# The opening of a decoder layer: identity turnings on TensorE before x arrives, each tile of x scaled behind its own root, and the norm's factors loaded behind the first four tiles

## The chip, the cores and the metric

The kernel runs on one NeuronCore of a Trainium2 chip. The metric is the device time of one execution in microseconds (us), as the median of several runs. All times in this document are in us unless ns is written. The engines are PE (TensorE, matrix products and transposes), ACT (ScalarE), DVE (VectorE), POOL (GpSimd) and SP (SyncE, which issues most of the transfers). Each engine works its own queue in order; a queue stops at an instruction whose operands aren't there, and everything behind it waits too.

## The reference

One layer of a hybrid decoder, on 1024 tokens of width 1024 behind 16 learned meta tokens:

```python
h = concat([pad, meta_tokens, x])
h = h + 0.5 * swiglu(rms_norm(h, ffn1_norm), ffn1_w_in, ffn1_w_out)     # first half-step FFN
u = rms_norm(h, mix_norm) @ w_in
o = concat([hgrn2(...u...), stick_breaking(...u...)])                  # two groups of heads
h = h + o @ w_out
h = h + 0.5 * swiglu(rms_norm(h, ffn2_norm), ffn2_w_in, ffn2_w_out)     # second half-step FFN
return h[:, pad + meta:, :]

def rms_norm(x, gain):
    return x * rsqrt(mean(x * x, axis=-1) + 1e-6) * gain
```

Only the first line of real work matters here: the norm of the first FFN, `rms_norm(h, ffn1_norm)`, and the first products with `ffn1_w_in`. Everything is float32 and is computed to about that accuracy.

## The kernel before, in words

**The whole.** The kernel goes through the layer in order: first FFN in, first FFN out, mixing norm and projections, the heads, `w_out`, second FFN. Every float32 product is made of three passes: each operand is split into a rounded high part and a low part, and PE multiplies high by high, low by high and high by low. The two FFN products of 512-token halves use a Strassen-like scheme over 2 x 2 blocks with seven products instead of eight; its block operands are called B11, B21, T1 to T4 and B22. A group of 12 matmuls (four slices of 128 in depth, three passes each) is one such block product of one weight block with one operand.

**The opening** (`open_tokens`, from line 790) makes the operands of the first FFN. x is 1024 x 1024; the first 512 tokens are four row tiles of 128 x 1024 (`ra[0]` to `ra[3]`), the others are `rb[0]` to `rb[3]`. For each row tile:

- `row_sum` (lines 757 to 764): the sum of squares along each row, on ACT (line 764, an activation and a read of its accumulator) or on DVE (line 761, the same in one product).
- `row_root` (lines 766 to 770): a square root on ACT (line 769) and a reciprocal on DVE (line 770).
- `row_scale` (lines 772 to 776): DVE multiplies the tile by it, in one piece or in two halves of 512 columns.

Then `turned` (lines 778 to 788) transposes on PE: for each row tile in order, each of the named column blocks, as a product with the identity (line 785), into PSUM tiles `xps` that hold one column block k of all four row tiles. `first(k, ...)` (lines 832 to 836) multiplies such a PSUM tile by the norm's factor `g[k]`, which is `ffn1_norm` laid out by partitions (`g1`, 128 x 8): ACT makes the rounded high part (line 835), DVE the low part (line 836). Column blocks 0 to 3 make B11, 4 to 7 make B21. Line 854 and `spare` (line 830) make a plain scaled copy (`b11`) of blocks 0 and 1, after which their PSUM tiles are free; the transposes of blocks 6 and 7 go to the same two PSUM banks.

**The weights' side.** `fast_in` (from line 350) gives generators, one for each of eight column tiles of `ffn1_w_in`. `order` lists them by pairs. The first and second `next` of a generator each make one weight operand: a load of a 256 KB block issued by SP (line 370), a cast to the high part on ACT (line 360), a difference to the low part on DVE (line 362). The third `next` does the first group of 12 matmuls (operand B11, line 450) and a copy of its result on ACT (line 474), the fourth the second group (operand B21). So `order[0]` and `order[1]` are the first weight blocks of the first two generators, `order[2]` and `order[3]` their second blocks.

**What sets the order.** In `open_tokens` the order on ACT, DVE and SP is that of the program text (a manual schedule), and on PE it is so through the whole stage. POOL's order, and ACT's, DVE's and SP's outside this function, is planned by the framework. SP issues transfers in text order too: the four tiles `ra`, two weight blocks, the four tiles `rb`, a third weight block, the meta tokens, and further weight blocks. Eight transfers of these queues can be in flight, since each takes one of eight semaphores; the issue after those waits for the landing of the transfer that had the semaphore before.

**Constants.** `setup` (from line 69) makes the identity (DVE memset, then line 79 on POOL), constants, and a first square root on ACT (line 87). It collects the small loads in a list; the first of them, g1, is issued at once on ACT's queue (line 104): 1024 elements of four bytes, each to its own place. `masks_blank` (line 120) fills a tile on DVE from which POOL cuts masks (lines 129 and 133). Line 1824 in `run` makes `ng1`, the negative of g1, on DVE; it is first read at line 879, some steps later (`combine`).

Of the kernel before, what the change touches and what calls it, by code (L numbers as in the profile page):

```python
# [11 lines left out]
F32 = mybir.dt.float32  # L12
# [8 lines left out]
P = 128  # L21
# [27 lines left out]
class Block:  # L49
# [19 lines left out]
    def setup(self):  # L69
        nc, a = self.nc, self.a  # L70
        self.loads = []
        self.const = c = self.pool("const")
        c.tile([P, 368], F32, name="base")
        self.pool("edge", side="right").tile([P, 504], F32, name="edge")
        self.dram = self.pool("scratch", space=DRAM)

        self.ident = c.tile([P, P], F32, name="ident")
        nc.vector.memset(self.ident, 1.0)
        nc.gpsimd.affine_select(
            out=self.ident, in_=self.ident, pattern=[[-1, P]],  # L80
            compare_op=ALU.is_equal, fill=0.0, base=0, channel_multiplier=1,
        )
        self.ones_d = c.tile([P, P], F32, name="ones_d")
        nc.vector.memset(self.ones_d, 1.0 / D)
        self.eps = c.tile([P, 1], F32, name="eps")
        nc.vector.memset(self.eps, EPS)
        nc.scalar.activation(c.tile([P, 1], F32, name="root"), self.eps, AF.Sqrt)

        self.g1 = self.column(a["ffn1_norm"][0], KT, "g1")
        self.gm = self.column(a["mix_norm"][0], KT, "gm")  # L90
        self.g2 = self.column(a["ffn2_norm"][0], KT, "g2")
        self.og = self.column(a["hgrn_out_norm"][0], 4, "og")
        self.l0 = self.column(a["hgrn_lb_logits"][0], 4, "l0")
        self.l1 = self.column(a["hgrn_lb_logits"][1], 4, "l1")
        self.qg, self.kg, self.qg8 = (c.tile([P, 1], F32, name=x) for x in ("qg", "kg", "qg8"))
        for h in range(2):
            s = slice(64 * h, 64 * h + 64)
            self.loads.append((self.qg[s], a["sb_q_norm"].rearrange("a d -> d a")))
            self.loads.append((self.kg[s], a["sb_k_norm"].rearrange("a d -> d a")))
        self.mx, self.lb, self.lbc = (c.tile([P, 4], F32, name=x) for x in ("mx", "lb", "lbc"))  # L100
        self.masks = c.tile([P, len(LEVELS), P], U8, name="masks")
        self.ss = c.tile([P, 9, 2], F32, name="ss_x")
        self.ng1 = c.tile([P, KT], F32, name="ng1")
        nc.scalar.dma_start(*self.loads.pop(0))

    def setup_rest(self):

# [682 lines left out]
    def open_tokens(self, ops, opened, prepare, rows_at, ev, operands):  # L790
# [9 lines left out]
        nc, x = self.nc, self.a["x"][0]  # L800
# [3 lines left out]
        junk = [rp.tile([P, D], (BF16, U8)[i], name=f"junk{i}") for i in range(2)]  # L804
        order = [q for i in range(0, len(opened), 2) for _ in range(2) for q in opened[i : i + 2]]

        def rows_in(r0):
            got = []
            for i in range(4):
                row = rp.tile([P, D], F32, tag="row", name="row", bufs=8)  # L810
                nc.sync.dma_start(row, x[r0 + i * P : r0 + i * P + P])
                got.append(row)
            return got
# [12 lines left out]
        kept = {}  # L826
# [5 lines left out]
        def first(*ks):  # L832
            for k in ks:
                hi, lo = (t[:, k % 4, :] for t in ops[("B11", "B21")[k // 4]])
                nc.scalar.mul(hi, kept[k], g[k])  # L835
                stt(lo, kept[k], g[k], hi.bitcast(F32), ALU.mult, ALU.subtract)  # L836

        ra = rows_in(0)
        self.masks_blank(sd)
        for i in range(3):  # L840
            self.row_sum(ra[i], i, junk, nc.vector if i == 1 else nc.scalar)
            self.row_root(ra[i], i)
        for i in range(3):
            self.row_scale(ra[i], i)
        self.row_sum(ra[3], 3, junk, nc.scalar)
        self.row_root(ra[3], 3)
        self.row_scale(ra[3], 3, 2)
        next(order[0])
        next(order[1])
        rb = rows_in(512)  # L850
        meta = rp.tile([META, D], F32, name="meta")
        kept.update(self.turned(ra, range(6), "bbccdd"))
        first(0, 1, 2, 3)
        nc.vector.tensor_scalar_mul(b11[0], kept[0], g[0])
        spare(1)
        next(order[2])
# [4 lines left out]
        next(order[1])  # L861
        kept.update(self.turned(ra, (6, 7), "bb"))
        first(6, 7)
        next(order[3])

        def turn_b22():
# [907 lines left out]
    def run(self):  # L1774
        nc, tc, a = self.nc, self.tc, self.a
# [20 lines left out]
        with ExitStack() as c0:  # L1796
            with ExitStack() as c1:
# [8 lines left out]
                with tc.manual_schedule(engines={nc.tensor.engine}), ExitStack() as c2:  # L1806
# [14 lines left out]
                    operands(xa, ("B11", "B21"))  # L1821
                    self.pin = self.pool("pin1", 1, PSUM, c2)
                    self.t_bufs, self.in_bufs = 2, 10
                    nc.vector.tensor_scalar_mul(self.ng1, self.g1, -1.0)

                    def ahead_of_time(pool):

# [66 lines left out]
                    first, hooks, steps_ahead = 32, 54, 58  # L1894
# [272 lines left out]
                with tc.manual_schedule(engines={nc.tensor.engine}):  # L2167
# [7 lines left out]
                    with ExitStack() as c2:  # L2175
                        self.att.append(self.pool("att1", ctx=c2))
                        tag = self.proj_tags[0]
# [214 lines left out]
```

## Time and profile before

| | |
|---|---|
| median of three runs | 1959.63 |
| the three runs | 1960.16, 1959.63, 1957.4 |
| the profiled execution | 1959.65 |
| its span, first to last instruction | 1957.9 |
| PE busy | 1919.8 (98% of the span) |
| DVE busy | 1390.4 (71%) |
| ACT busy | 849.6 (43%) |
| POOL busy | 450.5 (23%) |

The 1.75 between the profiled execution's time and its span lie around the instructions. Where rows of the profile are quoted, they read as follows. In a timeline: start in us from the span's start, duration, engine, line of the kernel, instruction, output<-input by the program's names, shape, how many in a row (x4), and in brackets how long the engine had been idle and who ended that. An engine with a q (SPq, ACTq) is its issue of a transfer. In the chain of waits: start, duration, engine, tile and line of the work that the end of the span depended on. In the view of one tile: line, engine, instruction, count, shortest/median/longest duration in ns, first and last start. In the table by stretches: the stretch, its length, busy time (and count) of PE, PE's weight loads, DVE, ACT and POOL, the clock of PE, the share of the transfer engines, GB/s. Matmul durations in the trace overlap; the rate is read from their starts.

The profile's first 40th (0 to 49 us) has PE busy for 7 tenths, every other 40th for 9 tenths or more. PE's first instruction starts at 11.

### The profile page before, as it was taken

To read this page: it belongs to the slowest core of one execution; us is meant where nothing else is said; L and a number is where in the kernel's file an instruction comes from. 1 tells how busy PE (TensorE), PEld (TensorE's weight loads), DVE (VectorE), ACT (ScalarE), POOL (GpSimd) and SP (SyncE) were. 2 spreads that over 40 slices of the span, in tenths; PEclk is the share of its full clock that TensorE was granted. 3 is DMA by queue.
4 is the path that set the end of the run, shared out by engine and by line. 5 is a ranking of instruction groups with operands and counts; after the bars stand their busy time and mean duration, and the time that the engine had idled before them with its cause. 6 is when DMAs were issued, how large, how long until landed. Compare 5 with 4: busy or idle time off the path is not lost.

```text
span 1957.9 us, 30218 instructions
## 1 busy us (share of the span) xinstructions
PE 1919.8 (98%) x10607; PEld 1616.6 (83%) x10607; DVE 1390.4 (71%) x2184; ACT 849.6 (43%) x1711; POOL 450.5 (23%) x625
## 2 busy tenths in 40 slices
PE   7999999999999999999999999999999999999999
PEld 6888888788888888888898978887888888888887
DVE  7977877877678665467777766677567767766774
ACT  6523443334444544356666635433232332344443
POOL 3010100001000003133333332210544645530000
PEclk9999999999999999999999999999999999999999
DMA  7356887758965315865454177655634444469473
GB/s 213 93 165 170 253 272 243 233 203 291 375 221 188 127 54 144 193 170 148 128 148 121 57 253 225 161 208 183 198 115 140 128 131 121 132 243 318 154 231 113
DMA packets 381687, 355.54 MB, mean 182 GB/s; under 512 B 129040, under 2 KB 284560, under 8 KB 381536
## 3 DMA queue, kind: packets, MB, share of 16 engines
q1 hardware_dynamic: 359728, 288.98, 48.7%
q0 software_dynamic: 20768, 64.63, 9.5%
q8 instruction: 84, 1.38, 0.3%
q14 instruction: 67, 0.55, 0.1%
q10 hardware_dynamic: 1040, 0.00, 0.0%
HBM read 237.95 MB, written 115.57 MB: 181 GB/s over the span
## 4 chain that ended last, share of the span: by engine, by line
PE 89%; DVE 4%; DMA 3%; ACT 2%; issue 1%; POOL 1%; SPq 1%; DVEq 0%; ACTq 0%; POOLq 0%
PE o L732 21%; PE qb L450 18%; PE qa L450 12%; PE qc L450 12%; PE proj L249 5%; PE proj L251 4%; PE proj L250 4%; PE flip L1495 2%; PE wo L250 1%; PE wo L249 1%; PE wo L251 1%; PE mq L1001 1%; PE oacc L1572 1%; PE oacc L1570 1%; DMA oT<-oD 1%
## 5 line engine op out<-in xcount | busy, mean ns | idle before, releaser
L450 PE MATMUL qb<-T,wh 128*128 128x512 f32 x1056 | 344.6, 390 | 1.3 <-ACT T L309 0.8
L450 PEld LDWEIGHTS qb<-T,wh 128*128 128x128 f32 x1056 | 198.1, 188 | 46.4 <-issue 2.5
L450 PE MATMUL qa<-B,wh 128*128 128x512 f32 x696 | 226.7, 390 | 0.3 <-ACT B L835 0.2
L249 PE MATMUL proj<-xh,wh 128*128 128x512 f32 (+2 forms) x640 | 213.2, 333 | 2.6 <-ACT st L1142 1.3
L732 PE MATMUL o<-t,w 128*128 128x512 f32 x924 | 211.8, 390 | 0.7 <-DVE u L543 0.7
L251 PE MATMUL proj<-xl,wh 128*128 128x512 f32 (+2 forms) x640 | 210.2, 328 | 0.8 <-DVE xl L1957 0.8
L250 PE MATMUL proj<-xh,wl 128*128 128x512 f32 (+2 forms) x640 | 210.1, 328 | 0.0
L732 PE MATMUL o<-parts 128*128 128x512 f32 x924 | 209.6, 389 | 0.0
L450 PE MATMUL qb<-T,wl 128*128 128x512 f32 x528 | 205.5, 389 | 0.0
L732 PEld LDWEIGHTS o<-t,w 128*128 128x128 f32 x924 | 172.8, 188 | 37.8 <-ACT sgm L981 1.1
L732 PEld LDWEIGHTS o<-parts 128*128 128x128 f32 x924 | 173.5, 188 | 36.0
L362 DVE TENSOR_TENSOR wl<-s,wh 128x512 fp32r<-128x512 f32 x160 | 165.6, 1035 | 50.8 <-ACT wh L360 49.9
L360 ACT CAST wh<-s 128x512 fp32r<-128x512 f32 x160 | 99.2, 622 | 188.5 <-PE qb L450 141.1
L450 PEld LDWEIGHTS qa<-B,wh 128*128 128x128 f32 x696 | 130.5, 188 | 28.0 <-DVE B L836 0.5
L360 ACT CAST wh<-raw 128x512 fp32r<-128x512 f32 x120 | 74.4, 621 | 155.8 <-PE qc L450 111.4
L450 PE MATMUL qa<-B,wl 128*128 128x512 f32 x348 | 135.4, 389 | 0.0
L249 PEld LDWEIGHTS proj<-xh,wh 128*128 128x128 f32 x640 | 120.8, 189 | 15.0 <-ACT st L1142 2.2
L251 PEld LDWEIGHTS proj<-xl,wh 128*128 128x128 f32 x640 | 120.7, 189 | 12.3 <-DVE xl L1957 1.2
L250 PEld LDWEIGHTS proj<-xh,wl 128*128 128x128 f32 x640 | 120.8, 189 | 10.1
L450 PE MATMUL qc<-B,wh 128*128 128x512 f32 x352 | 115.1, 390 | 2.3 <-DVE u L543 2.3
L450 PE MATMUL qc<-T,wh 128*128 128x512 f32 x352 | 117.0, 394 | 0.0
L450 PEld LDWEIGHTS qb<-T,wl 128*128 128x128 f32 x528 | 99.1, 188 | 20.2
(393 smaller groups left out, 3819.4 us busy)
## 6 DMA issues: line engine op xcount, KB each, us to landing
raw<-in_ffn_w_in_dram SPq DMA_DIRECT2D x176, 256.0 KB, 4.0
raw<-in_ffn_w_out_dram SPq DMA_DIRECT2D x112, 256.0 KB, 4.5
w2in<-both SPq DMA_DIRECT2D x28, 512.0 KB, 3.4
raw<-in_w_in_dram SPq DMA_DIRECT2D x25, 512.0 KB, 5.2
ks<-kD SPq DMA_DIRECT2D x32, 260.0 KB, 4.8
wout<-both SPq DMA_DIRECT2D x16, 512.0 KB, 3.7
wh<-w2in SPq DMA_DIRECT2D x27, 256.0 KB, 3.1
wl<-w2in SPq DMA_DIRECT2D x27, 256.0 KB, 3.1
```

The costliest lines, as they stand in the source:

```text
L249: nc.tensor.matmul(ps, wh[:, s], xs, start=k == 0, stop=False)
L250: nc.tensor.matmul(ps, wl[:, s], xs, start=False, stop=False)
L251: nc.tensor.matmul(ps, wh[:, s], xl[:, k, c0 : c0 + n], start=False, stop=k == nk - 1)
L360: nc.scalar.copy(hi, src)
L362: self.block_lo = nc.vector.tensor_sub(lo, src, hi.bitcast(F32))
L450: nc.tensor.matmul(ps, a[:, k, :], b[:, k, :], start=start and k == 0 and i == 0, stop=k == 3 and i == 2, skip_group_check=True,)
L732: nc.tensor.matmul(banks[bank][m], y[:, m * P : (m + 1) * P], z, start=start and at == 0 and e == 0, stop=q == nq - 1 and e == 2, skip_gro ...
L1001: nc.tensor.matmul(ps[at : at + 32, :], self.xm[:, 4 * h + k, :], got[i, h][:, k, :], start=h == 0 and k == 0, stop=h == 1 and k == 3, til ...
L1495: self.nc.tensor.transpose(ps[:m, j, :], src[:, s0 : s0 + m], self.ident)
L1570: nc.tensor.matmul(o[:, c], vj, w[0], start=j == 0, stop=False, skip_group_check=True)
L1572: nc.tensor.matmul(o[:64, c], vj[:, :64], w[1], start=False, stop=end, skip_group_check=True)
```

## The change

- g1's load leaves ACT's queue in `setup` and becomes SP's fifth issue, behind the four tiles `ra` and ahead of the first weight block.
- PE gets 30 transposes of the identity at the head of its queue, into the four quarters of one PSUM tile (`warm`, one of the two buffers of tag `qd`), whose content nobody reads.
- The sums: tiles 0, 1 and 3 are now summed on ACT and tile 2 on DVE (before: 0, 2 and 3 on ACT, 1 on DVE). Each tile is scaled right behind its own root, not after all three roots.
- The first weight operand of the second generator (`order[1]`) and the loads of `rb` come in the text behind the turning of column blocks 0 to 5 and `first(0, 1, 2, 3)`, not ahead of them: on ACT and DVE its cast and its low part are now queued behind the four B11 products, and ahead of `b11`. On SP the order of the loads stays.
- `ng1` is made after `first(6, 7)` and no longer at line 1824.

```diff
@@ setup
         self.ng1 = c.tile([P, KT], F32, name="ng1")
-        nc.scalar.dma_start(*self.loads.pop(0))
@@ open_tokens
         ra = rows_in(0)
+        nc.sync.dma_start(*self.loads.pop(0))
+        warm = self.pin.tile([P, 512], F32, tag="qd", name="warm", bufs=2)
+        for i in range(30):
+            nc.tensor.transpose(warm[:, P * (i % 4) : P * (i % 4) + P], self.ident, self.ident)
         self.masks_blank(sd)
-        for i in range(3):
-            self.row_sum(ra[i], i, junk, nc.vector if i == 1 else nc.scalar)
+        for i in range(2):
+            self.row_sum(ra[i], i, junk, nc.scalar)
+            if i == 1:
+                self.row_sum(ra[2], 2, junk, nc.vector)
             self.row_root(ra[i], i)
-        for i in range(3):
             self.row_scale(ra[i], i)
+        self.row_root(ra[2], 2)
+        self.row_scale(ra[2], 2)
         self.row_sum(ra[3], 3, junk, nc.scalar)
         self.row_root(ra[3], 3)
         self.row_scale(ra[3], 3, 2)
         next(order[0])
+        kept.update(self.turned(ra, range(6), "bbccdd"))
+        first(0, 1, 2, 3)
         next(order[1])
         rb = rows_in(512)
         meta = rp.tile([META, D], F32, name="meta")
-        kept.update(self.turned(ra, range(6), "bbccdd"))
-        first(0, 1, 2, 3)
         nc.vector.tensor_scalar_mul(b11[0], kept[0], g[0])
@@ open_tokens, further down
         kept.update(self.turned(ra, (6, 7), "bb"))
         first(6, 7)
+        nc.vector.tensor_scalar_mul(self.ng1, self.g1, -1.0)
         next(order[3])
@@ run
                     self.t_bufs, self.in_bufs = 2, 10
-                    nc.vector.tensor_scalar_mul(self.ng1, self.g1, -1.0)
```

## The prediction, made before the change was built

> **What bounds the kernel now.** I read the page first, then the chain of waits for the first 48 us, then the timelines of ScalarE (ACT) and VectorE (DVE), then single tiles and transfers.
>
> ```profile
> span 1957.9 us, 30218 instructions
> ...
> PE 89%; DVE 4%; DMA 3%; ACT 2%; issue 1%; POOL 1%; SPq 1%; DVEq 0%; ACTq 0%; POOLq 0%
> ```
> ```profile
> 11.01 3.69 PE xps L785 x19
> ...
> 14.73 0.70 ACT B L835
> ...
> 15.45 0.76 DVE B L836
> ...
> 18.84 1.03 PE xps L785 x8
> 19.87 16.37 PE qa L450 x72
> ```
>
> The chain is TensorE (PE) for 89% of the span, so whatever time PE gains at the start is kept if nothing later makes it wait. PE turns (transposes) its first tile of x at 11.01; ACT (14.73) and DVE (15.45) then make the first operand of the products; two columns of tiles are turned at 18.84, and from 19.87 the row of 72 matmuls has no pause. The change can act on these 20 us only. What fills them:
>
> ```profile
> 4.55 1.06 ACT L764 ACTIVATE junk<-row 128x1024 bf16<-128x1024 f32 x1 [1.75 <-DMA row<-in_x_dram]
> ...
> 8.33 0.29 ACT L769 ACTIVATE ss_x<-ss_x,eps 128x1 f32<-128x1 f32 x1 [2.30 <-DVE junk L761]
> 8.53 1.04 ACT L764 ACTIVATE junk<-row 128x1024 bf16<-128x1024 f32 x1
> ...
> 9.70 0.29 ACT L769 ACTIVATE ss_x<-ss_x,eps 128x1 f32<-128x1 f32 x1
> ...
> 11.06 0.29 ACT L769 ACTIVATE ss_x<-ss_x,eps 128x1 f32<-128x1 f32 x1
> ...
> 14.73 2.43 ACT L835 ACTIVATE B<-xps,g 128x512 fp32r<-128x512 f32 x4 [2.34 <-PE xps L785]
> ...
> 17.60 0.64 ACT L360 CAST wh<-raw 128x512 fp32r<-128x512 f32 x1
> ```
> ```profile
> 7.06 1.22 DVE L761 SCALAR_TENSOR_TENSOR junk<-row 128x1024 uint8<-128x1024 f32 x1 [0.76 <-DMA row<-in_x_dram]
> ...
> 10.02 0.16 DVE L770 RECIPROCAL ss_x<-ss_x 128x1 f32<-128x1 f32 x1 [1.20 <-ACT ss_x L769]
> 10.11 2.08 DVE L776 TENSOR_SCALAR row<-row,ss_x 128x1024 f32<-128x1024 f32 x3
> 12.11 0.15 DVE L770 RECIPROCAL ss_x<-ss_x 128x1 f32<-128x1 f32 x1
> 12.30 0.88 DVE L776 TENSOR_SCALAR row<-row,ss_x 128x512 f32<-128x512 f32 x2
> ...
> 15.45 2.72 DVE L836 SCALAR_TENSOR_TENSOR B<-xps,g,B 128x512 fp32r<-128x512 f32 x4 [0.99 <-ACT B L835]
> ...
> 18.75 0.68 DVE L362 TENSOR_TENSOR wl<-raw,wh 128x512 fp32r<-128x512 f32 x1
> ...
> 22.42 1.40 DVE L836 SCALAR_TENSOR_TENSOR B<-xps,g,B 128x512 fp32r<-128x512 f32 x2
> ```
>
> Row tile 0 is in SBUF at 4.5 and tile 1 at 7.06, and still the first scaling starts at 10.11: all three scalings are queued on DVE behind the third root. The fourth tile follows at 12.30. The waits view puts PE's first wait on POOL's masks; they feed nothing here, and what PE waits for is the scaling of 10.11.
>
> ```profile
> L785 PE MATMUL xps<-ident,row x13: 421/421/447, 11.0 to 13.6; 128*128 128x128 f32 x13
> ```
> ```profile
> 41.20 1.75 PE xps L785 x16
> ```
>
> The first transposes follow each other at 2.6/12 = 0.217 us, later ones at 1.75/16 = 0.109: PE starts at half speed. So before the change PE's 24 turnings, most of them slow, and not DVE hand the first operand to ACT at 14.73.
>
> **Part by part.** First the factors g1. They left ACT's queue beside the rows:
>
> ```profile
> 3.00:3.50 0.50, 0.00 (x0) 0.00 (x0) 0.00 (x0) 0.00 (x0) 0.50 (x2) 1.00 1.05 410
> 3.50:4.50 1.00, 0.00 (x0) 0.00 (x0) 0.00 (x0) 0.00 (x0) 1.00 (x4) 1.00 0.90 114
> 4.50:5.50 1.00, 0.00 (x0) 0.00 (x0) 0.00 (x0) 0.95 (x1) 1.00 (x3) 1.00 0.95 320
> ```
> ```profile
> q10 hardware_dynamic: 1040, 0.00, 0.0%
> ```
>
> The last column is GB/s. While 1040 packets of four bytes pass, the engines move 114 and 320 instead of 410: (296 + 90)/410 = 0.94 us of row traffic lost. Behind the rows, this is lost after row 3 instead; rows 1 to 3 land 0.94 earlier, and everything behind g1 when it did. The landings (SP's issues, then the transfer view of three single issues, whose last number is the time from issue to landing: row 3, the first and the third weight block):
>
> ```profile
> 0.82 2.06 SPq L811 DMA_DIRECT2D row<-in_x_dram  x4
> 2.92 1.14 SPq L370 DMA_DIRECT2D raw<-in_ffn_w_in_dram  x2
> ...
> 8.36 0.38 SPq L370 DMA_DIRECT2D raw<-in_ffn_w_in_dram  x1
> ```
> ```profile
> row<-in_x_dram SPq DMA_DIRECT2D x1, 512.0 KB, 7.4
> ```
> ```profile
> raw<-in_ffn_w_in_dram SPq DMA_DIRECT2D x1, 256.0 KB, 7.4
> ```
> ```profile
> raw<-in_ffn_w_in_dram SPq DMA_DIRECT2D x1, 256.0 KB, 8.7
> ```
>
> Row 3, the last of the four issues that end at 2.88, goes out at 2.2 and lands 7.4 later, at 9.6; the first weight block (call it w0) at 2.92 + 7.4 = 10.3; the third (w2), which is behind the other four rows, at 8.36 + 8.7 = 17.06. After: rows 1, 2, 3 at about 6.1, 7.4, 8.7; g1 by 9.6; w0 and w2 unchanged at 10.3 and 17.06. SP gets one more issue in front of w0, some 0.5 us (four rows take 2.06); it has been issuing 7 us ahead of the landings, so this is hidden, unless the queue runs empty. The 1024 descriptors may also cost nothing (w0, w2 0.9 earlier) or twice (0.9 later); I take the same, since it is the same load.
>
> Scaling, in the order of the new code. ACT sums row 1 at 6.1 (sum to root 1.17, from 8.53 and 9.70). DVE sums row 2 from 7.4, and the root and scaling of row 1 are queued behind it: root 1.27 later (7.06 to 8.33), at 8.67. Nobody waits for row 1, since row 3 is last. ACT's sum of row 3 stands behind that root: 8.87; its root at 10.04. DVE does rows 1 and 2 meanwhile, 0.67 each (2.08 for three), and is free at about 10.3; reciprocal 0.32 after the root (9.70 to 10.02), and scaling 0.19 after that: 10.56, where it was 12.30. First half done at 11.0.
>
> The 30 turnings of the identity need only the identity:
>
> ```profile
> 1.80 0.29 POOL L79 TENSOR_SCALAR_AFFINE_SELECT ident<-ident 128x128 f32<-128x128 f32 x1
> ```
> ```profile
> L785 PE MATMUL xps<-ident,row x12: 272/273/421, 13.6 to 15.0; 128*128 128x128 f32 x12
> ```
>
> They run from 2.1 to 8.6 at the latest (30 x 0.217), all in idle time; row 0, scaled some 2.3 after its landing at 4.5, may wait until then; row 3 comes at 11.0. They cost nothing on the path. What they buy is that row 3's turnings are fast and that rows 0 to 2 are already through. Turnings alone brought PE to speed in this trace: their durations fall from 421 to 273 ns at 13.8, before any matmul. The Trainium skill says otherwise (TensorE: Matmul & The Clock Gate, Part 4: PE-mode transpose): in transpose mode the full clock doesn't engage, since it doesn't count as PE-busy in the same way. By that rule the turnings buy nothing; the trace disagrees here, and I keep a rival for it.
>
> ACT's first B comes after the last tile's first half, one turning (0.273) and two hand-overs of some 0.1 (DVE's own from 10.02 to 10.11 is 0.09): 11.47 instead of 14.73, 3.26 earlier. ACT has cast w0 just before (10.3 to 10.9), and g1 is there. DVE's first product follows 0.72 later (14.73 to 15.45), at 12.19.
>
> Here the moved step costs. Before, DVE did five operations of 0.66 from 15.45 to 18.75: four products and b11, for which the turnings of columns 6 and 7 wait. Now the second block's low part stands between them, so b11 ends after six, at 16.15 against 18.75, and PE does these turnings 2.60 earlier, not 3.26.
>
> ```profile
> 19.63 0.47 PE L450 MATMUL qa<-B,wh 128*128 128x512 f32 x1
> ```
> ```profile
> 20.67 1.21 DVE L761 SCALAR_TENSOR_TENSOR junk<-row 128x1024 uint8<-128x1024 f32 x1
> ```
>
> So the second group of 12 starts at 17.03 and, at 16.37/72 = 0.227 each, the third group at 19.76. That one needs all of B21. But ACT's cast of w2 stands before the four remaining B products in its queue, and w2 lands at 17.06: the cast of 17.60 gains only 0.54. DVE's low part of w2 follows at about 17.65 instead of 18.75, and behind it DVE works without a pause, the sum of row 4 (20.67) among it, up to the product of 22.42: 3.67 behind that low part as before, so at 21.32, and ready at 22.02. The third group's ninth matmul would want it at 19.76 + 8 x 0.227 = 21.58 and waits 0.44. From there PE is 2.60 - 0.44 = 2.16 ahead, say 2.1. Behind that the chain is PE without a pause, so ACT and DVE keep up, and they move with it. ng1, moved behind the last product, is one DVE operation on 8 columns, between nothing and the 0.68 that one on 512 takes, and PE pays nothing while DVE is ahead; ACT's freed issue slot at 0.81 saves nothing, since ACT waits 1.75 for row 0 anyway.
>
> Sum: the profiled execution took 1959.65, its span 1957.9 and 1.75 around it; the median of the three runs is 1959.63, so one baseline serves. 1959.6 - 2.1 = **1957.5**. Bounds of the unknown load: w2 0.9 earlier gives the full 2.6 (1957.0); w2 0.9 later moves the wait by as much, gain 1.2 (1958.4).
>
> **Rivals.** *Behind the opening.* The order on ACT and DVE after these tiles isn't written out but planned, and a shift of the opening may reorder it. One of PE's longest waits by the waits view (total, times, longest) shows what that is worth:
>
> ```profile
> PE qc L450 <- DVE u L543: 2.3, 3, 1.5
> ```
>
> One or two such waits more undo the gain (1959.6); a few less give 1955. For it: nothing but that they exist. Against: they lie hundreds of microseconds behind.
>
> *Weights not binding.* If the small packets pass quicker in one queue with the rows, w2 comes before ACT asks for it, and PE keeps 2.6, or 3.2 where DVE's extra low part finds a gap: 1956.7.
>
> *Turnings don't speed PE up* (the rule above). Then 30 + 18 slow ones keep PE busy until 2.1 + 48 x 0.217 = 12.5, the first B comes at 13.0, 1.5 later than in my sum, and some eight of the first matmuls take twice 0.227, 1.8 more. The two waits of 0.66 and 0.44 vanish in that: 3.26 - 1.5 - 1.8 + what overlaps leaves a gain of at most 0.5, so 1959.1. The fall at 13.8 speaks against it.
>
> *Slower: the identity's turnings get in the way.* All 30 go to one PSUM tile and stand first in PE's queue. If each waited out the one before (447 ns), they would end at 2.1 + 30 x 0.447 = 15.5; 18 fast turnings (1.96) and 0.47 later B starts at 17.9, 3.2 later than before: 1962.8. It decides from 0.34 us each on, where they end at 12.3. Against it:
>
> ```profile
> 45.71 0.60 PE mps L888 x8
> ```
>
> Eight turnings into one tile went at 0.075 each.
>
> **How the numbers follow.** Chances: forecast 0.62; weights not binding 0.12; not sped up 0.06; behind the opening lost 0.07, and won 0.07; in the way 0.06. A measurement of this kernel tells about 0.2%, 3.9 us, from no change. The forecast, the not-sped-up and the lost case lie within that; the won case, a little of weights and the spread of the runs (1957.4 to 1960.16) pass it downwards: 0.14. In the way, and as much from the spread, passes it upwards: 0.06. The forecast's own range is 1957.0 to 1958.4; with half the runs' spread on each side and the cases next to it, 1955.2 to 1960.2.
>
> **What would show it.** Right: the first scaling near 6.1 and not 10.1, ACT's first B near 11.5, PE's second group near 17.0, ACT's cast of w2 starting on a landing near 17.06, a pause of about 0.4 in the group after it, and the same order with a shift of 2.1 from then on. Wrong: transposes of 421 ns for row 3; identity turnings that last beyond 11; w0 landing later than 11.3 (SP held up by g1), behind which ACT's first B would queue; or a PE that is ahead by 2 at 30 us and not at the end.

## The result, and the profile after

| | median | runs | spread |
|---|---|---|---|
| before | 1959.13 | 7 | 1956.74 to 1960.16 |
| after | 1964.18 | 7 | 1963.44 to 1968.36 |

The change makes the kernel slower: ratio 1.0031, 95% interval 1.0022 to 1.004. The forecast was 1957.5 with a range up to 1960.2. The profiled execution of after took 1966.7, its span is 1964.9.

The opening is close to what the prediction described. ACT's and PE's timelines of after:

```profile
11.67 2.42 ACT L834 ACTIVATE B<-xps,g 128x512 fp32r<-128x512 f32 x4 [0.77 <-PE xps L784]
...
17.82 0.62 ACT L359 CAST wh<-raw 128x512 fp32r<-128x512 f32 x1 [2.63 <-DMA raw<-in_ffn_w_in_dram]
```
```profile
2.13 5.89 PE L841 MATMUL warm<-ident 128*128 128x128 f32 x30 [2.13 <-POOL ident L79]
...
12.41 0.50 PE L449 MATMUL qa<-B,wh 128*128 128x512 f32 x1 [0.23 <-ACT B L834]
...
16.43 0.98 PE L784 MATMUL xps<-ident,row 128*128 128x128 f32 x7 [0.55 <-DVE b L860]
17.17 0.48 PE L449 MATMUL qa<-B,wh 128*128 128x512 f32 x1
...
22.94 0.73 PE L449 MATMUL qa<-B,wh 128*128 128x512 f32 x2 [0.70 <-DVE B L835]
```

The first B starts at 11.67 instead of 14.73, the second group of matmuls at 17.17 instead of 19.63. So PE is ahead and not behind when the opening ends. To see where that goes I paired the 10607 matmuls and turnings that both traces have in order and took the difference of their starts (the lead of after). The lead changes at few places:

| at (before's clock) | lead of after | what stands there |
|---|---|---|
| 15.5, first matmul | 3.06 | |
| 18.9, columns 6 and 7 | 2.46 | b11 after six DVE operations, not five |
| 24.3 | 1.35 | ACT waits for w2, DVE's B is late |
| 222 and 262 | 0.87, then -0.52 | a weight load lands late, twice |
| 385 | -0.97 | |
| 470.6, first FFN-out product | -5.55 | PE waits 5.0 for DVE |
| 471 to 474 | -8.09 | PE at half clock |
| end | -6.97 | before has a half-clock stretch of its own near 868 |

(This pair of executions differs by 7.0 and the medians by 5.1, since the profiled execution of after lies 2.5 above its median.) Nearly all of the loss lies at 470, where the first FFN's input products end and its output products (`o`) begin. After's group, its waits and its chain there, in this order:

```profile
L731 PE MATMUL o<-t,w 128*128 128x512 f32 x924 | 214.3, 393 | 5.0 <-DVE actm L989 5.0
```
```profile
PE o L731 <- DVE actm L989: 5.0, 1, 5.0
```
```profile
471.00 1.28 DVE u L542 x2
472.28 0.07 DVE sg L543
472.35 0.45 issue
472.80 0.68 DVE sum L200
473.48 0.60 DVE both L180
474.08 0.12 DVE sg L543
474.20 0.41 issue
474.61 0.15 DVE both L180
474.76 0.45 issue
475.21 0.68 DVE t L561
475.89 0.11 DVE actm L989
476.00 0.14 issue
476.14 11.88 PE o L731 x40
```

The same place before, in its chain, where PE waits for one product of DVE:

```profile
469.76 0.69 DVE u L543
470.45 0.14 issue
470.59 17.50 PE o L732 x76
```

`actm` is a short product of the meta tokens (0.11 of the chain) that stands in DVE's queue behind the eight operations ahead of it in this chain. The matmul doesn't use its result: `o<-t,w`. What can connect them is PSUM. `actm` is the last reader of the tile `mf`, and `mf` has the tag `qd`, the same as `warm`. The stretches around the stall (length, then busy time of the engines, and behind the count of POOL the granted clock of PE), before and after:

```profile
460.00:470.00 10.00, 9.85 (x89) 7.90 (x77) 6.54 (x13) 5.08 (x12) 0.47 (x1) 1.00 0.99 322
476.00:483.00 7.00, 7.00 (x33) 5.77 (x32) 5.86 (x10) 3.19 (x6) 1.29 (x3) 1.00 1.03 386
```
```profile
460.00:470.00 10.00, 10.00 (x101) 8.20 (x100) 6.31 (x12) 5.63 (x12) 0.00 (x0) 1.00 0.96 331
476.00:483.00 7.00, 6.86 (x19) 5.48 (x20) 3.11 (x5) 0.37 (x1) 2.16 (x4) 0.60 1.01 387
```

Before has the full clock of 1.00 and runs 33 matmuls in these 7 us; after has 0.60 and runs 19. The pause costs a second time.

### The profile page after: what moved, and what is told of

Its sections match the earlier page's. It is cut to its first block, busy times and chain, and to the rows that moved or that the text cites. A ratio compares the mean times of both kernels' runs of the same rounds, so it can differ in the third digit from the quotient of the medians.

```text
span 1964.9 us, 30276 instructions
## 1 busy us (share of the span) xinstructions
PE 1927.2 (98%) x10637; PEld 1620.9 (82%) x10637; DVE 1391.2 (71%) x2184; ACT 849.0 (43%) x1711; POOL 448.2 (23%) x625
## 4 chain that ended last, share of the span: by engine, by line
PE 87%; DVE 5%; DMA 3%; ACT 2%; issue 1%; SPq 1%; POOL 0%; DVEq 0%; ACTq 0%; POOLq 0%
PE o L731 21%; PE qb L449 17%; PE qa L449 12%; PE qc L449 12%; PE proj L248 4%; PE proj L250 4%; PE proj L249 4%; DMA raw<-in_ffn_w_in_dram 2%; PE flip L1502 2%; PE wo L249 1%; PE wo L248 1%; PE wo L250 1%; PE mq L1008 1%; PE oacc L1579 1%; PE oacc L1577 1%
```

## The experiments

**Two theories of the stall.** *Place* supposes that PSUM banks go to tags in the order of their first use. Before, the order of first use was qb, qc, qd, qa; `warm` makes qd the first. If the next stage's output tiles are laid over the banks that come first, they now lie where `mf` was and must wait for `actm`. *Turn*: qd has two buffers, and one extra tile shifts which of the two each later tile of the tag gets. *Order* (the prediction's rival "behind the opening") is already out: on ACT, DVE and POOL the instructions behind the opening stand in the same order in both kernels.

**e1_qd_twice** splits the turnings over two qd tiles, so that every later tile has its old buffer again.

```diff
-        warm = self.pin.tile([P, 512], F32, tag="qd", name="warm", bufs=2)
+        warm = [self.pin.tile([P, 512], F32, tag="qd", name="warm", bufs=2) for _ in range(2)]
         for i in range(30):
-            nc.tensor.transpose(warm[:, P * (i % 4) : P * (i % 4) + P], self.ident, self.ident)
+            at = P * (i % 4)
+            nc.tensor.transpose(warm[i // 15][:, at : at + P], self.ident, self.ident)
```

> The change with its 30 identity turnings split over two PSUM tiles of the tag qd, so that later tiles of qd fall on the same of its two buffers as before the change; qd is still the first tag to be used. Theory (place): the tag that is used first gets the first PSUM banks; qd's banks then become the first output banks of the next stage, whose first products must wait for the last reader of qd, the small product actm at the end of DVE's queue. So the pause of about 5 us at the change of stage (470 us) and the stretch at half clock behind it stay: 1964. Rival (turn): the one extra tile swapped the two buffers of qd; then the pause is gone: 1957. Rival (time): the earlier opening moved the engines against each other; then nothing changes: 1964.

**e2_qb_twice** is the same with `tag="qb"`, the tag that comes first anyway.

> The change with its 30 turnings in two PSUM tiles of the tag qb instead of one of qd: qb is then used first, as before the change, and all buffers come round as before. Place and turn both expect no pause at 470 us, at most the 0.7 that was there before the change, full clock behind it, and the opening's lead as in the changed kernel (1.4 us at 24 us): 1957 to 1959, by how much of that lead is still there at 460 us. Time expects the pause of 5 us as in the changed kernel: 1964.

**e3_before_qd_first** is before with one turning of the identity into a qd tile ahead of everything, and nothing else.

```diff
         ra = rows_in(0)
+        warm = self.pin.tile([P, 512], F32, tag="qd", name="warm", bufs=2)
+        nc.tensor.transpose(warm[:, :P], self.ident, self.ident)
```

> The kernel before with one thing added: a single turning of the identity into a tile of the tag qd ahead of all other PSUM tiles; the opening stays as it was. Place (and turn): the pause of 4 to 5 us at the change of stage and a stretch at half clock behind it appear, without any of the change's gains: 1964 to 1966. Time: nothing happens, 1959.

**e4_no_turnings** is after without `warm` and its 30 turnings.

> The change without the 30 turnings; all the rest of it is there. Place: qb is used first again, so there is no pause at 470 us. The opening: if the turnings bring PE to full clock, the row tiles' turnings and the first matmuls run at half speed here (transposes of 421 ns) and the lead at 24 us is 0.5 to 1 us smaller than with them, unless the wait for the third weight block covers it: 1958 to 1959. If the turnings don't matter, the transposes of the last row tile are at 273 ns as with them. Time: pause as in the changed kernel, 1964.

Measured on one chip, with before at 1958.85 (24 runs). The ratios here and below come from all the runs and aren't quotients of the medians.

| | median | ratio, 95% interval | wait of `o` for `actm` |
|---|---|---|---|
| e1_qd_twice | 1965.41 | 1.0032 (1.0020 to 1.0044) | 4.8 |
| e2_qb_twice | 1960.27 | 1.0003 (0.9995 to 1.0012) | none (0.7 for `u`, as before) |
| e3_before_qd_first | 1964.61 | 1.0026 (1.0015 to 1.0037) | 5.0 |
| e4_no_turnings | 1957.30 | 0.9992 (0.9983 to 1.0001) | none (0.7 for `u`) |

The waits view of e3_before_qd_first, and its stretch behind the stall:

```profile
PE o L732 <- DVE actm L984: 5.0, 1, 5.0
```
```profile
476.00:483.00 7.00, 7.00 (x23) 5.58 (x24) 2.76 (x5) 0.94 (x2) 1.99 (x4) 0.71 1.03 407
```

One turning of half a microsecond, 460 us earlier, brings the whole stall and the low clock into a kernel that is otherwise before. With the old turns restored (e1) the stall stays, and between e1 and e2 the tag alone is worth 5.1 us. So it is shown that the tag that is used first decides, and turn is refuted as the cause. That the earlier opening moved the engines against each other (*time* in the expectations) is out too: the opening of e3 is 0.9 later than before's and the stall is there, the opening of e2 is 3 earlier and it isn't. The turn still shows, in e1:

```profile
470.47 0.48 PE L731 MATMUL o<-t,w 128*128 128x512 f32 x1
475.76 2.47 PE L731 MATMUL o<-t,w 128*128 128x512 f32 x5 [4.80 <-DVE actm L990]
```

Here the first `o` starts at once and the second waits, where in after and in e3 the first waits. That fits two buffers of qd lying under the first two output tiles. No view shows addresses, so that it goes by banks is argued from the kernel's text and from these waits.

**Second question.** Without the stall the turnings still don't pay: e2_qb_twice is ahead by 2.98 at columns 6 and 7, e4_no_turnings, whose turnings of rows run slowly, only by 1.32, and yet e4 ends 3 us earlier. Both missed their ranges, e2 above and e4 below. Two theories. *w2 late*: ACT's cast of the third weight block waits longer the more PE is ahead. *Fetch phase*: PE's program is fetched by DMA in pieces of 16 KB (the queue "instruction" in the profile); 30 turnings are 60 more instructions in front, with the weight loads of PE, so the fetches come at other moments and hit other transfers.

**e5_w2_first** is e2_qb_twice with the loads of `rb` behind w2's, **e6_w2_first_no_turnings** the same move in e4_no_turnings:

```diff
         next(order[1])
-        rb = rows_in(512)
-        meta = rp.tile([META, D], F32, name="meta")
         nc.vector.tensor_scalar_mul(b11[0], kept[0], g[0])
         spare(1)
         next(order[2])
+        rb = rows_in(512)
+        meta = rp.tile([META, D], F32, name="meta")
```

> The kernel of qb_twice (turnings in two qb tiles, 1960.3), with the four loads of the other rows and the meta tile moved in the text behind the third weight block w2, so that w2 is the sixth transfer of SP and not the tenth. Two theories of why qb_twice, ahead by 3 at 16 us, ends 3 later than the version without turnings. 'w2 late': the lead is lost where ACT waits for w2 (cast at 18.4 behind a wait of 3.7, PE pauses of 1.07 and 0.69). Then w2 lands near 12, its cast waits for nothing, PE is ahead by 2.5 or more at 24 us, and the end is about 1957.0 to 1958.0. 'Fetch phase': 60 more instructions on PE move the points at which PE's program is fetched, so that a fetch falls between the packets of the fourth store of act13T and act14T, which then lands 4.5 after its issue instead of 2.6; DVE's products wait 1.5 to 2.2 for it and PE pauses at 221 and 262. Then those stores still take 4 to 5, and of the lead of 2.5 some 2 is lost at these two places: 1958.5 to 1960. Third: the other rows now land too late and DVE's sum of row 4 (about 20) holds up the B21 products: lead below 1 at 30 us.

> The version without the 30 turnings (1957.3) with the same move of the loads. 'w2 late' expects w2's cast without a wait, and since PE is slow here until 15 and its lead at columns 6 and 7 is 1.3, a lead of 1.3 to 1.9 at 24 us and about 1957. 'Fetch phase' expects the fourth stores of act13T and act14T to land in 2.5 to 2.8 and no loss at 221 and 262, so that this one ends 1 to 3 before w2_first, although it starts with a smaller lead: 1956.5 to 1957.5. If it ends within 1 of w2_first, the fetch phase explains nothing.

**e7_w2_first_wide** has four wide products in place of e5's 30 turnings.

```diff
-        for i in range(30):
-            at = P * (i % 4)
-            nc.tensor.transpose(warm[i // 15][:, at : at + P], self.ident, self.ident)
+        wide = self.ident.unsqueeze(1).broadcast_to([P, 4, P])
+        for i in range(4):
+            nc.tensor.matmul(
+                warm[i // 2].rearrange("p (a b) -> p a b", a=4), self.ident, wide, start=True, stop=True
+            )
```

> The kernel of w2_first with the 30 turnings replaced by four products of the identity with four copies of it side by side (128x512, float32), two in each of two qb tiles: PE is busy for about as long, with some 8 instructions instead of 60. 'Fetch phase': PE's fetches stay within 1 us of where they are without turnings, the fourth stores of act13T and act14T land in 2.5 to 2.8, the lead of 2.5 or more is kept through 221 and 262, and the end is 1955.5 to 1956.5, the best of all. If PE's instruction count has nothing to do with it, stores are late and the end is as w2_first's, within 0.7. If wide products bring PE less speed than turnings, its first transposes of rows take 421 ns and the lead at 16 us is 1.3 instead of 3.

**e8_before_turnings_qb** is before with e2's 30 turnings and nothing else.

> Before, with the 30 turnings alone, in two qb tiles; nothing else is changed. They end by 8.6; the turnings of rows start at 10.95 as before but are fast, so ACT's first B comes at about 12.9 to 13.2 instead of 14.73 (row 3 is scaled from 12.30 still). 'w2 late': w2's cast at 17.6 behind landing 17.06, so a lead of 0.6 to 1.5 at 24 us, and the end is that much before: 1957.5 to 1958.3. 'Fetch phase': the stores of act13T or act14T land in 4 to 5 and 1 to 2 is lost at 221 and 262: 1958.5 to 1960. The layout theory expects no stall at 470, since qb has the first banks as before.

Measured, with before at 1958.42 (33 runs): e5 1960.42, ratio 1.0007 (0.9998 to 1.0016); e6 1957.48, 0.9992 (0.9983 to 1.0001); e7 1956.37, 0.9996 (0.9987 to 1.0005); e8 1961.62, 1.0014 (1.0005 to 1.0023).

In e5 ACT casts w2 at 14.58 without waiting, PE has no pause after 16.7, and the lead at 30 us is 2.69 where e2 had 0.61. The end is the same as e2's. So w2 costs lead, as the prediction feared, but that lead is lost later anyway: *w2 late* doesn't explain the end. e8 shows the turnings doing harm alone, and above its range: it is 0.6 behind at 24 us already and loses 0.9 more at 221 and 1.7 at 262.

**e9_wide_and_small** replaces the fourth wide product of e7 by 26 small turnings, **e10_16_turnings** has 16 turnings in e5 instead of 30.

```diff
-        for i in range(4):
+        for i in range(3):
...
+        for i in range(26):
+            at = META * i
+            nc.tensor.transpose(
+                warm[1][:, at : at + META], self.ident[:META, :], self.ident[:META, :META]
+            )
```

> w2_first_wide (1956.4) with the fourth of its four wide products replaced by 26 small turnings of the identity's first 16 rows: the same end of the idle turnings within 1 us, the same speed for the rows' turnings, but 58 instructions more on PE than without turnings, as the 30 turnings are 60. 'Fetch phase': PE's program is fetched at 241 instead of 243.9, inside the fourth store of act14T, which lands in 4.3 to 5 instead of 2.6; DVE waits some 1.5 for it, PE's lead drops by 1.2 to 1.8 at 262 and the end is 1 to 3 later than w2_first_wide's 1956.4 (a span of 1955.5 to 1957). If the number of instructions doesn't matter and it was the kind of turning, no loss at 262 and the end is as w2_first_wide's within 0.7.

> w2_first (30 turnings in two qb tiles, 1960.4) with 16 turnings instead of 30. 'Fetch phase': 28 instructions fewer, the fetch that fell at 241.0 falls 1 to 2 later, just behind the fourth store of act14T (which would end near 241.3), so that this one lands in 2.6 to 3.2 and nothing is lost at 262: the end 1.2 to 1.8 before w2_first's. On the clock: the 16 turnings end near 5.5 and rows start at 7.3; in before_turnings_qb an idle time of 3.2 put PE back to turnings of 421 ns and kept it there for 5.4 us, without turnings it took 6.7. If a pause of 1.8 does the same, ACT's first B comes near 12.9 as without turnings; if not, near 11.2.

Measured, with before at 1959.12 (21 runs): e9 1958.01, ratio 0.9996 (0.9988 to 1.0005); e10 1956.32, 0.9990 (0.9981 to 0.9999). (The wide products are two instructions on PE each, with as many weight loads: e7 has 16 more than e6 and e9 64, not 8 and 58.)

The late fourth stores of act14T come about as expected (4.3 to 4.8 in the six kernels with 60 or 64 more instructions, 2.6 or 2.7 in the others). Those of act13T don't quite: e7 and e10 have them too (4.90 and 4.47), and e1 hasn't (2.61). But the late stores are not what PE waits for: in every kernel DVE has been idle for 2.9 us or more when it takes up the loads of the table below, and that idle time takes the delay up. The chain names another transfer, a load of weights. Around 262, e7 and then e9:

```profile
254.97 2.95 PE qc L449 x12
257.92 2.72 PE qb L449 x12
260.64 2.72 PE qc L449 x12
```
```profile
256.36 1.02 PE mq L1016 x32
257.38 5.55 DMA raw<-in_ffn_w_in_dram
262.93 0.02 issue
262.96 0.70 DVE s L381
...
264.48 0.63 ACT wh L359
265.11 0.01 issue
265.12 0.93 PE qc L449 x3
```

SP issues these loads when PE has let go of what they need (254.10 in e7, 257.38 in e9), so they can't start earlier, however far ahead DVE is. The transfers of e7 between 254.1 and 258.0, and of e9 between 257.4 and 262.9 (queue, packets, MB, share):

```profile
q1 hardware_dynamic: 1585, 0.89, 87.3%
```
```profile
q1 hardware_dynamic: 2587, 1.39, 91.3%
q8 instruction: 1, 0.02, 2.4%
```

A fetch of 16 KB passes in e9 while the load is on its way, and none in e7. The engines as a whole weren't slower in e9: 1.39 MB in 5.5 us against 0.89 in 3.9. The same for all kernels, at both places: the start of the fetch nearest to the load, and the time from SP's issue of the load to DVE's first subtraction on it; * marks a fetch that lies between the two.

| | fetch | issue to use, 221 | fetch | issue to use, 262 |
|---|---|---|---|---|
| before | 224.7 | 4.00 | 263.9 | 4.04 |
| e3_before_qd_first | 225.1 | 4.22 | 265.2 | 3.96 |
| e4_no_turnings | 222.4 | 3.95 | 262.8 | 4.00 |
| e6_w2_first_no_turnings | 222.9 | 4.15 | 262.6 | 4.10 |
| e7_w2_first_wide | 216.3 | 4.63 * | 262.1 | 3.92 |
| e10_16_turnings | 215.8 | 5.04 * | 262.7 | 3.91 |
| after | 216.1 | 4.63 * | 256.9 | 5.48 * |
| e1_qd_twice | 217.0 | 4.38 * | 258.0 | 5.26 * |
| e2_qb_twice | 217.1 | 4.69 * | 258.4 | 5.51 * |
| e5_w2_first | 216.0 | 6.15 * | 257.9 | 5.35 * |
| e8_before_turnings_qb | 218.6 | 4.99 * | 260.0 | 5.93 * |
| e9_wide_and_small | 214.6 | 6.46 * | 259.2 | 5.58 * |

In these 24 places there is no exception: 3.91 to 4.22 without a fetch, 4.38 to 6.46 with one. Every marked fetch starts within 3.3 us of the issue, so it isn't just that a longer load has more time to meet one. At 262 the lead drops by 1.1 to 1.8 in the six kernels with 60 or 64 more instructions, and by less than 0.1 in the five others.

But the two places were picked because the lead dropped there, and at other places where DVE takes up such a load the same count separates nothing. From issue to landing, the loads issued near 337 take 4.5 to 5.2 with a fetch on the way (before, e3, e4 and e6) and 4.7 to 5.1 without one in seven others. Those issued near 378 take 3.9 to 4.8 with one and 3.7 to 4.6 without. In e2 the load at 338, without a fetch, takes 3.29; PE has no pause there, and e2 gets back 1.8 of its lead between 262 and 380.

So at 221 and 262 a fetch goes with a late load of weights, and it isn't the stores that PE waits for, as I had expected. That the fetch holds the load up is not shown, and neither is that it decides the ends: the trace doesn't say which of the 16 engines a packet took, and the later loads speak against a general rule. Nor is it settled why the load is 0.4 late in one case and 2.4 in another. In e9 the pause at 221 is followed by half clock from 222.4 to 225.9, which takes another 1.6 of its lead; its profile is of its slowest run (1961.84 where the median is 1958.01). The Trainium skill (Runtime: NRT & Kernel Launch, Instruction fetch mechanics) states that an engine's sequencer fetches its program in blocks of 16 KiB, 256 instructions, while it executes the block before, and calls the cost "mostly hidden". The size agrees: q8 moves 84 such packets for PE's 21,274 instructions in after. Whether it stays hidden from a load beside it, these runs leave open. In times the pair e7 and e9 doesn't tell the theory apart, since both have the ratio 0.9996; e5 against e10 (1.0007 and 0.9990) goes its way, with intervals that just overlap.

On the clock, e8 missed its expectation. The timelines of PE in e8 and in e10:

```profile
2.13 5.74 PE L842 MATMUL warm<-ident 128*128 128x128 f32 x30 [2.13 <-POOL ident L79]
11.04 5.36 PE L785 MATMUL xps<-ident,row 128*128 128x128 f32 x24 [3.16 <-DVE row L776]
```
```profile
2.13 3.34 PE L842 MATMUL warm<-ident 128*128 128x128 f32 x16 [2.13 <-POOL ident L79]
7.27 0.85 PE L784 MATMUL xps<-ident,row 128*128 128x128 f32 x6 [1.80 <-DVE row L775]
9.30 4.10 PE L784 MATMUL xps<-ident,row 128*128 128x128 f32 x18 [1.19 <-DVE row L775]
```

In e8 the speed is gone after 3.16 of idle time: all 24 turnings of rows are slow, and PE is 0.9 behind before when they are done, not 1.5 ahead as expected. In e10 the first six are still fast after 1.80, and the next 18, another 1.19 later, are slow. In after the gaps are 0 and 1.07, and all stay fast. The granted clock (behind POOL's count) says the same of e10:

```profile
4.98:8.39 3.41, 1.33 (x10) 0.88 (x8) 2.21 (x5) 2.41 (x6) 3.41 (x7) 1.00 1.05 343
8.39:15.22 6.83, 5.92 (x23) 5.33 (x24) 5.46 (x12) 4.98 (x11) 5.78 (x18) 0.50 0.98 331
```

The lowest median is that of e10_16_turnings: 1956.32, ratio 0.9990, the only interval that lies below 1, and only just. One such among ten variants can be chance, and e7 is at 1956.37. The opening of e10 isn't the fastest (first B at 12.38), but it has neither the stall nor the late load at 262.

## Why the prediction was wrong

**The step that failed** is "They cost nothing on the path", of the 30 turnings. Their time on PE was priced rightly: they end by 8.0, in idle time. Their tile was not priced. It makes qd the tag that is used first, and that changes what the next stage's outputs must wait for. e3_before_qd_first, before with that alone, puts it at a wait of 5.0 where before waits 0.7, another 2.0 through the half clock, and 5.8 between the medians. The list of what was taken and moved had "one PSUM tile" in it, and I asked who writes to it, but not who has that place next.

**"Behind the opening"** had 0.07 for a loss, with 1959.6. The mechanism it named, a reordered plan, didn't happen. What spoke against it, "they lie hundreds of microseconds behind", was no argument: the stall lies 450 us behind. The prediction's own sign for being wrong, PE ahead at 30 us and not at the end, is what came, with 1.2 for the 2.

**"Behind that the chain is PE without a pause, so ACT and DVE keep up, and they move with it"** failed as well, on a smaller scale. At 221 and 262 a weight load issued at PE's release is on the path, and the lead falls from 1.30 to -0.52. DMA's 3% of the chain were in the page.

**w2**, 17.06 "unchanged": it came at 17.8, near the bound of 0.9 later. The extra issue was not hidden. SP's timeline of after, where before has 1.14 for the two weight blocks and 8.36 for w2:

```profile
2.65 0.56 SPq L838 DMA_DIRECT2D g<-in_ffn_norm_dram  x1
3.25 2.41 SPq L369 DMA_DIRECT2D raw<-in_ffn_w_in_dram  x2
5.70 4.16 SPq L810 DMA_DIRECT2D row<-in_x_dram  x4
9.90 0.94 SPq L369 DMA_DIRECT2D raw<-in_ffn_w_in_dram  x1
```

Behind g1's issue, SP takes 2.41 for w0 and w1; it does so in e4_no_turnings too (2.44), and not in e8 (1.11), which has the turnings but g1 on ACT. The pause was 0.70 where 0.44 was forecast, the lead 1.35 where 2.1 was.

**Right** were the first scaling (6.26 for 6.1), row 3's scaling (10.68 for 10.56), the first B (11.67 for 11.47), the second group (17.17 for 17.03), w0 in time (its cast starts at 10.29), the cast of w2 on a landing, and that the identity's turnings don't stand in each other's way. The Trainium skill's rule that the full clock doesn't engage in transposes (TensorE: Matmul & The Clock Gate, Part 4: PE-mode transpose) is contradicted once more: the turnings of the identity fall from 417 to 273 ns at 6.9, and the granted clock is 1.00 from 7.08 on, with no other work on PE before them.

## What to carry to other kernels

A scratch tile is a change of layout. Before taking one, ask which tag or bank it moves and who gets that place in the next stage; the wait can appear hundreds of microseconds later, named after an instruction that has nothing to do with the waiting one, and a tag that is first in use anyway was the safe choice here. A lead won at the start can be lost at any transfer that PE itself releases, so small gains should be followed matmul by matmul to the end of the trace.

## What the runs showed of the hardware

- The pause of 5 us at PE is followed by half clock in all three kernels that have it, for 5.4 us in after, 5.8 in e1_qd_twice and 4.2 in e3_before_qd_first: in after 13 matmuls take 5.55 from 476.14 on, and 3.03 before (0.43 and 0.23 each). It cost 2.5 in after, 2.8 in e1 and 2.0 in e3.
- How long PE needs to speed up varies: the granted clock becomes 1.00 2.9 us after the first turning in before (11.01 to 13.93), 4.9 after it in after (2.13 to 7.08), 4.1 in e2_qb_twice (2.13 to 6.28) and 6.0 after the second start in e8_before_turnings_qb (11.04 to 17.02). In e3, whose opening is before's but for the one turning, it takes 4.5 (11.29 to 15.81), and the first product comes 0.9 later, of which a start 0.3 later is a part. The way down takes less than a long pause: in e10_16_turnings the clock falls at 8.39, behind 3.41 us in which PE works for 1.33 and no gap is longer than 1.80. In each of the twelve executions the changes of the clock lie whole multiples of 3.41 apart, such as 13.93, 867.26 and 870.67 in before. The Trainium skill (TensorE: Matmul & The Clock Gate, Part 1) counts activity in free-running windows of some 3.4 us, one busy window for the way up and one idle window for the way down. The multiples of 3.41 and the spread on the way up agree with windows that run freely; on the way down these runs show that the window need not be idle throughout.
- 16 more instructions on PE, with PE some 1.2 further ahead, move a fetch from 222.9 to 216.3 (e6 and e7), and 44 more (e5) only from there to 216.0: the moments of the fetches don't move evenly with the count.
